# Accumulating transfers, split means and later loads in a hybrid encoder block

## The chip, the cores and the metric

The kernel runs on one NeuronCore of a Trainium2 chip. The metric is the device time of one execution in microseconds. Engines are named as in the profile: PE is TensorE (PEld its weight loads), DVE is VectorE, ACT is ScalarE, POOL is GpSimd and SP is SyncE. SP, ACT and POOL each issue DMA transfers in the order of their own queue, and the 16 DMA engines of the core move the bytes.

## The reference

One layer for 1024 tokens of 1024 channels, all in float32: two token mixers side by side with a gated merge, then a squared-ReLU MLP, with a root-mean-square norm before and after each.

```python
h = rmsnorm(x, g_pre_mix)
u_pool, q, k, v = split(h @ w_in)            # 512 channels each; 8 heads of 64
# pooling: group g of 128 channels, window w = 2, 4, 8, 16
pooled = trailing_mean(u_pool[g], w) - u_pool[g]
y_pool = concat(pooled @ w_pool_mix[g]) * pool_scale @ w_br_pool
# stick-breaking attention, strictly causal
z = q @ k.T / 8
A[t, s] = sigmoid(z[t, s]) * prod(1 - sigmoid(z[t, j]) for s < j < t)
y_sb = (A @ v) @ w_br_sb
gates = sigmoid(h @ w_gate + b_gate)
merged = gates[:, :1024] * y_pool + gates[:, 1024:] * y_sb
x = x + rmsnorm(merged @ w_out, g_post_mix)
h2 = rmsnorm(x, g_pre_mlp)
x = x + rmsnorm(relu(h2 @ w_up) ** 2 @ w_down, g_post_mlp)
```

## The kernel before

**Layout and precision.** Channels lie on the 128 partitions and tokens on the free dimension, in two halves h of 512 tokens. Each float32 operand is split into a high part (a cast, on ACT) and a low part (source minus high part, on DVE), and every product is three matmuls of 128x512 into one PSUM bank: high by high, high by low and low by high (`mm3`, L104 to L106; L102 where attention pins the order).

**Order of the work.** The program is written in one order, and a planner with a cost model of its own fixes each engine's queue at build time: it takes an instruction when, by its reckoning, the operands and the slot are there, so that a queue can differ from the written order. On the chip each queue runs strictly in its fixed order. `issue_after` ties an instruction behind another one of the same engine. Tiles with one tag share a fixed number of slots, and a new tile waits until the old one's readers are through, DMAs among them. The tags m0 to m3 of the pool `mx` are four such slots of 128x1024.

**Stages.** (1) Norm of x, u and v projections. (2) `phase_project`: gates, q and k, twelve pairs of weight blocks, each pair as seven half-size block products (`product`, 12 matmuls) with sums on DVE. `result` ends each block: gates are stored straight from the result's tile on ACT's queue, q and k are scaled and split into a staging tile (slots m0 and m1 in turn) and stored from POOL's queue, q with its high part twice. Beside it runs `later`, advanced by one step per product: per pooling group it loads u, adds up windows on DVE, takes the mean, splits it (`ph`, `pq`), multiplies it and stores the split result; then it prepares v. Partial sums of the down weights are formed in DRAM by copying and accumulating transfers from POOL (`weight_sums`), released a piece at a time: 12 behind u, 16 in the projections, 12 in attention. (3) `phase_attention`: for each half of the tokens (g) eight heads; scores on PE, sigmoid on ACT, a scan on DVE, transposes on PE, a split on ACT and DVE, and products with v. Between them `pump` mixes in other matmul steps, as many per head as `deal` says: `job_pool` (branch product times gate, stored as `bscr`), `job_merge` (the other branch times its gate, plus `bscr`) for the first half, and `job_out`. (4) `phase_post`: `job_merge` for the second half, the out projection, and `chain` beside it: norm, residual added, stored as `xscr`, squares, next norm and the split of the MLP's operands. (5) `phase_mlp`: the up products in two passes; the first stores partial results (`pscr`), the second loads them back in quarters (`quarter`) and combines seven block products per pair of weights (`pair_weights`). `down` does the same with the down weights, loading its first operands early.

## Time and profile before

| What | Value |
|---|---|
| median of three runs | 1279.97 us (1277.24 to 1282.58) |
| profiled execution, its own time | 1283.02 us |
| its span | 1281.1 us |
| instructions | 16198 |
| mean granted TensorE clock | 0.997 |
| bytes moved by DMA | 283 MB |

In rows of instructions an arrow points from the operand to the result ("T<-z" reads z and writes T); a bracket gives the idle time of the engine just before and what ended it. Lines such as L897 are lines of the kernel before. "SPq" and "ACTq" rows are the issue of a DMA. Matmuls are pipelined, so their single durations overlap. A wait for several semaphores is put down to the one that came last.

### The profile page before, as it was taken

To read this page: it belongs to the slowest core of one execution; us is meant where nothing else is said; L and a number is where in the kernel's file an instruction comes from. 1 tells how busy PE (TensorE), PEld (TensorE's weight loads), DVE (VectorE), ACT (ScalarE), POOL (GpSimd) and SP (SyncE) were. 2 spreads that over 40 slices of the span, in tenths; PEclk is the share of its full clock that TensorE was granted. 3 is DMA by queue.
4 is the path that set the end of the run, shared out by engine and by line. 5 is a ranking of instruction groups with operands and counts; after the bars stand their busy time and mean duration, and the time that the engine had idled before them with its cause. 6 is when DMAs were issued, how large, how long until landed. Compare 5 with 4: busy or idle time off the path is not lost.

```text
span 1281.1 us, 16198 instructions
## 1 busy us (share of the span) xinstructions
PE 1247.4 (97%) x5707; PEld 1022.0 (80%) x5707; DVE 970.6 (76%) x1311; ACT 621.9 (49%) x994; POOL 179.3 (14%) x319
## 2 busy tenths in 40 slices
PE   9999989999989999999999999999999999999998
PEld 6887768887877877777778878888888888888887
DVE  8759687776588898777777978888865564776985
ACT  7247344333455556554556635545554443344452
POOL 1212112342101011101101002221221110001000
PEclk9999999999999999999999989999999999999999
DMA  6586878977898774346638756766549997556552
GB/s 217 167 228 173 247 185 252 327 244 240 324 314 315 236 222 137 80 109 220 216 123 286 216 203 224 252 218 242 198 164 318 302 305 241 197 197 246 185 202 67
DMA packets 110306, 283.00 MB, mean 221 GB/s; under 512 B 12465, under 2 KB 17585, under 8 KB 109073
## 3 DMA queue, kind: packets, MB, share of 16 engines
q1 hardware_dynamic: 65696, 165.28, 37.2%
q0 software_dynamic: 30992, 91.13, 25.4%
q10 hardware_dynamic: 13536, 25.57, 6.1%
q8 instruction: 45, 0.74, 0.2%
q14 instruction: 37, 0.29, 0.1%
HBM read 208.52 MB, written 94.37 MB: 236 GB/s over the span
## 4 chain that ended last, share of the span: by engine, by line
PE 59%; DVE 8%; DMA 3%; issue 2%; ACT 2%; ACTq 0%; DVEq 0%; SPq 0%
PE d L104 16%; PE d L106 16%; PE d L105 16%; PE o L830 2%; DVE T L791 2%; PE dbr L106 2%; PE dbr L105 2%; PE dbr L102 2%; PE at L804 2%; DMA wraw<-w 1%; DVE wlo L75 1%; DVE alo L815 1%; DMA gt<-gscr 1%; PE z L787 1%; PE z L784 1%
## 5 line engine op out<-in xcount | busy, mean ns | idle before, releaser
L105 PE MATMUL d<-blo,whi 128*128 128x512 f32 (+1 forms) x456 | 172.3, 378 | 0.0
L106 PE MATMUL d<-bhi,wlo 128*128 128x512 f32 (+1 forms) x456 | 171.9, 378 | 0.0
L104 PE MATMUL d<-bhi,whi 128*128 128x512 f32 (+1 forms) x456 | 168.7, 378 | 0.0
L105 PEld LDWEIGHTS d<-blo,whi 128*128 128x128 f32 x456 | 85.7, 188 | 16.1
L106 PEld LDWEIGHTS d<-bhi,wlo 128*128 128x128 f32 x456 | 85.8, 188 | 15.8
L104 PEld LDWEIGHTS d<-bhi,whi 128*128 128x128 f32 x456 | 85.5, 188 | 16.0
L791 DVE TENSOR_TENSOR_SCAN T<-T,past 128x256 f32<-128x256 f32 (+5 forms) x64 | 84.5, 1347 | 5.8 <-ACT T L789 5.5
L105 PE MATMUL d<-b_lo,whi 128*128 128x512 f32 x196 | 76.3, 390 | 0.5 <-DVE b_lo L1060 0.5
L104 PE MATMUL d<-b_hi,whi 128*128 128x512 f32 x196 | 75.3, 391 | 0.6 <-ACT b_hi L1059 0.6
L106 PE MATMUL d<-b_hi,wlo 128*128 128x512 f32 x196 | 74.8, 390 | 0.0
L75 DVE TENSOR_TENSOR wlo<-wraw,whi 128x1024 fp32r<-128x1024 f32 x45 | 54.9, 1219 | 24.4 <-ACT whi L74 24.4
L74 ACT CAST whi<-wraw 128x1024 fp32r<-128x1024 f32 x45 | 47.4, 1054 | 49.6 <-DMA wraw<-w 17.1
L814 ACT CAST ahi<-at 128x512 fp32r<-128x512 f32 (+1 forms) x96 | 44.6, 483 | 48.5 <-PE at L804 40.2
L815 DVE TENSOR_TENSOR alo<-at,ahi 128x512 fp32r<-128x512 f32 (+1 forms) x96 | 50.7, 549 | 19.8 <-ACT ahi L814 19.5
L1351 DVE TENSOR_TENSOR wlo<-slots_hi,whi 128x1024 fp32r<-128x1024 f32 x29 | 35.5, 1224 | 37.7 <-ACT whi L1349 37.6
L1349 ACT CAST whi<-slots_hi 128x1024 fp32r<-128x1024 f32 x29 | 30.5, 1052 | 68.5 <-PE d L105 62.3
L1349 ACT CAST whi<-slots_lo 128x1024 fp32r<-128x1024 f32 x27 | 28.4, 1054 | 63.4 <-PE d L105 53.1
L104 PE MATMUL sw<-h_hi,whi 128*128 128x512 f32 x144 | 56.5, 393 | 2.0 <-ACT vs L619 0.8
L105 PE MATMUL sw<-h_lo,whi 128*128 128x512 f32 x144 | 56.1, 389 | 0.0
L106 PE MATMUL sw<-h_hi,wlo 128*128 128x512 f32 x144 | 55.5, 390 | 0.1
L104 PE MATMUL d<-t_hi,whi 128*128 128x512 f32 x132 | 52.7, 399 | 2.5 <-ACT whi L1166 2.5
L789 ACT ACTIVATE T<-z 128x256 f32<-128x256 f32 (+3 forms) x96 | 44.3, 500 | 19.9 <-PE z L787 10.9
(443 smaller groups left out, 3425.7 us busy)
## 6 DMA issues: line engine op xcount, KB each, us to landing
wraw<-w SPq DMA_DIRECT2D x57, 512.0 KB, 4.9
ext_b<-ascr SPq DMA_DIRECT2D x40, 512.0 KB, 7.1
wscr<-w POOLq DMA_DIRECT2D x32, 512.0 KB, 8.9
slots_hi<-w SPq DMA_DIRECT2D x10, 1024.0 KB, 7.7
slots_lo<-w SPq DMA_DIRECT2D x10, 1024.0 KB, 8.4
qq<-qscr SPq DMA_DIRECT2D x32, 256.0 KB, 5.9
pscr<-p SPq DMA_DIRECT2D x32, 256.0 KB, 4.5
u<-pscr ACTq DMA_DIRECT2D x32, 256.0 KB, 4.6
```

Source lines behind the costliest of these rows:

```text
L74: nc.scalar.copy(hi, raw)
L75: self.last_lo = nc.vector.tensor_sub(lo, raw, hi.bitcast(F32)).ins
L102: nc.tensor.matmul(ps, wh, rh, start=first and i == 0, stop=False)
L104: nc.tensor.matmul(ps, wh, rh, start=first and i == 0, stop=False)
L105: nc.tensor.matmul(ps, wh, rl, start=False, stop=False)
L106: self.last_mm = nc.tensor.matmul(ps, wl, rh, start=False, stop=last and i == n - 1).ins
L789: self.after = nc.scalar.activation(f, z[:, :n], AF.Sigmoid, scale=-1.0)
L791: nc.vector.tensor_tensor_scan(f[:, ::-1], f[:, ::-1], past[:, ::-1], 1.0, ALU.mult, ALU.max)
L814: nc.scalar.copy(hi[:, c:], at[:, c:])
L815: nc.vector.tensor_sub(lo[:, c:], at[:, c:], hi[:, c:].bitcast(F32))
L1349: last_split[0] = nc.scalar.copy(hi, src).ins
L1351: last_split[1] = nc.vector.tensor_sub(lo, src, hi.bitcast(F32)).ins
```

## The change

- `result`: the high parts of two results of q and k share one staging tile; the low part is written over the result itself, and each part is stored by a transfer of its own (q: six of 128 KB, k: four, for two heads).
- `later`: u of the next group is loaded before the mean is formed; window slots go on alternating over the groups; the mean is split and multiplied in two halves of 512 tokens, each half's parts in one tile; the results are stored from ACT's queue.
- Weight sums: the pieces released in the projections end at the 36th product; four more go to the last heads of attention.
- The first gate tiles of attention are fetched ahead of the y loads.
- `job_merge`: the term from `bscr` is no longer loaded and added on DVE; a transfer from POOL's queue accumulates it into the product's tile. The loads of the second half's gates get other slots, and `deal` changes for the second half.
- `chain`: x is no longer loaded; a transfer from POOL accumulates it into the normed tile, and what follows runs three channels behind.
- `phase_mlp`: quarters 0 and 1 are issued on ACT behind given casts, and the first load of the down operands on SP behind the third pair's weights.

```diff
         self.op7, self.sw, self.heads = {}, {}, {}
+        self.stage = []
         self.phase_in()
...
         sc = sign * (0.125 if kind == "q" else 1.0)
-        e = self.staged([P, 2, H], F32R, f"{kind}s")
-        nc.scalar.activation(e[:, 0, :], t, AF.Copy, scale=sc)
+        if not self.stage:
+            e = self.staged([P, 2, H], F32R, f"{kind}s")
+            self.stage = [e[:, 0, :], e[:, 1, :]]
+        hi = self.stage.pop(0)
+        nc.scalar.activation(hi, t, AF.Copy, scale=sc)
         nc.vector.scalar_tensor_tensor(
-            out=e[:, 1, :], in0=t, scalar=sc, in1=e[:, 0, :].bitcast(F32), op0=ALU.mult, op1=ALU.subtract
+            out=t.bitcast(F32R), in0=t, scalar=sc, in1=hi.bitcast(F32), op0=ALU.mult, op1=ALU.subtract
         )
+        parts = (hi.bitcast(F32), t, hi.bitcast(F32)) if kind == "q" else (hi.bitcast(F32), t)
         for b in range(2):
-            scr, s = self.qscr[kind == "k"][2 * f + b], e[64 * b : 64 * b + 64].bitcast(F32)
-            nc.gpsimd.dma_start(scr[0:128, c].rearrange("(n p) c -> p n c", n=2), s)
-            if kind == "q":
-                nc.gpsimd.dma_start(scr[128:192, c], s[:, 0, :])
+            scr = self.qscr[kind == "k"][2 * f + b]
+            for n, e in enumerate(parts):
+                nc.gpsimd.dma_start(scr[64 * n : 64 * n + 64, c], e[64 * b : 64 * b + 64])
 
...
         yield
+        n = 1
         for g in range(4):
-            iu = 3 * (g % 2)
-            u = nxt_u
-            cur, n = u, 0
+            u = cur = nxt_u
             for i in range(g + 1):
                 sh = 1 << i
-                n = 1 + i % 2
                 nxt = whole(n, name="win")
...
                 nc.vector.tensor_copy(nxt[:, :sh], cur[:, :sh])
-                cur = nxt
+                cur, n = nxt, 3 - n
                 yield
+            if g < 3:
+                nxt_u = u_load(g + 1)
             w = 1 << (g + 1)
...
             sc = self.vt[:, V_PSC + g : V_PSC + g + 1]
-            ph, pq = whole(3 - n, F32R, "ph"), whole(3 - iu, F32R, "pq")
-            nc.scalar.copy(ph, cur)
-            nc.vector.tensor_sub(pq, cur, ph.bitcast(F32))
-            yield
-            yield
-            ds = [self.zps.tile([P, H], F32, name="dm", tag="o", bufs=1), newbank()]
-            for h, d in enumerate(ds):
+            for h in range(2):
                 c = slice(h * H, h * H + H)
-                self.mm3(d, [(wmh[:, g, :], wml[:, g, :], ph[:, c], pq[:, c])])
+                pp = self.mx.tile([P, 2, H], F32R, name="pp", tag=f"m{n}")
+                ph, pq = pp[:, 0, :], pp[:, 1, :]
+                nc.scalar.copy(ph, cur[:, c])
+                nc.vector.tensor_sub(pq, cur[:, c], ph.bitcast(F32))
+                yield
+                d = newbank() if h else self.zps.tile([P, H], F32, name="dm", tag="o", bufs=1)
+                self.mm3(d, [(wmh[:, g, :], wml[:, g, :], ph, pq)])
                 nc.scalar.activation(cur[:, c].bitcast(F32R), d, AF.Copy, scale=sc)
...
                 )
-            if g < 3:
-                nxt_u = u_load(g + 1)
+            yield
             yield
             for t, scr in zip((cur, u), self.yscr):
-                nc.gpsimd.dma_start(scr[:, g, :], t)
-            yield
+                nc.scalar.dma_start(scr[:, g, :], t)
             yield
...
                 next(bg, None)
-            if c % 3 == 2 and c < 48:
+            if c % 3 == 2 and c < 36:
                 self.sum_piece_with(self.last_mm)
...
         self.fetch_order, self.fetches = jobs, {}
+        with tc.issue_after(self.head_load):
+            self.fetch(1)
         last = self.head_load
...
                 if h == 0:
-                    self.fetch(1)
                     self.load_head(1, 0, self.mx)
...
             else:
-                self.fetches[key] = self.staged_in(self.gscr[8 + e][:, c]), self.staged_in(self.bscr[e][h])
+                self.fetches[key] = self.staged_in(self.gscr[8 + e][:, c])
 
...
                 if g or h > 3:
-                    self.sum_pieces(zero, 1)
+                    self.sum_pieces(zero, 1 + (g and h > 3))
             nc.scalar.copy(hi[:, c:], at[:, c:])
...
             self.fetch(self.fetch_order.index(("m", e, 0)) + 1)
-            t, q = self.fetches["m", e, 0]
+            t = self.fetches["m", e, 0]
         else:
-            room = {2: ("T1", 6), 3: ("T0", 5), 4: ("ahi", 4), 5: ("alo", 4)}.get(e)
-            t, q = (self.staged_in(s, room) for s in (self.gscr[8 + e][:, c], self.bscr[e][h]))
+            room = {4: ("T1", 6), 5: ("T1", 6), 6: ("T0", 5), 7: ("T0", 5)}.get(e)
+            t = self.staged_in(self.gscr[8 + e][:, c], room)
         for k in range(4):
...
         nc.vector.tensor_mul(t, t, d)
-        nc.vector.tensor_add(t, t, q)
+        nc.gpsimd.dma_start(t, self.bscr[e][h], accum_op=ALU.add)
         if h not in self.mg:
...
         out = None
-        deal = [[5] * 4 + [4] * 4, [18, 18, 16, 11, 11, 11, 11, 12]]
+        deal = [[5] * 4 + [4] * 4, [16, 16, 14, 12, 12, 12, 13, 13]]
         for g in range(2):
...
         nc = self.nc
-        xr = []
-        for i, n in enumerate(("hi", "lo")):
-            t = self.hp.tile([P, 4, H], F32, name=f"xr{h}_{n}", tag=f"t4_{n}")
-            for j in range(2):
-                (nc.sync if h else nc.gpsimd).dma_start(t[:, 2 * j : 2 * j + 2, :], self.x[h][:, 4 * i + 2 * j : 4 * i + 2 * j + 2, :])
-            xr += [t[:, j, :] for j in range(4)]
         tmp = self.hp.tile([P, 4, H], F32, name=f"tmp{h}", tag="t3_hi")
...
         acc2 = ch.tile([P, H], F32, name="acc2", bufs=1)
-        for e in range(8):
-            yield 6 - early + 3 * e
+        for n in range(11):
+            if n < 8:
+                yield 6 - early + 3 * n
+                m = mix[n]
+
+                with self.tc.issue_after(self.last_lo):
+                    nc.vector.scalar_tensor_tensor(
+                        out=m, in0=m, scalar=self.gn[:, V_POST_MIX + n : V_POST_MIX + n + 1], in1=r,
+                        op0=ALU.mult, op1=ALU.mult,
+                    )
+                nc.gpsimd.dma_start(m, self.x[h][:, n, :], accum_op=ALU.add)
+            e = n - 3
+            if e < 0:
+                continue
             m = mix[e]
-
-            with self.tc.issue_after(self.last_lo):
-                nc.vector.scalar_tensor_tensor(
-                    out=m, in0=m, scalar=self.gn[:, V_POST_MIX + e : V_POST_MIX + e + 1], in1=r,
-                    op0=ALU.mult, op1=ALU.mult,
-                )
-                nc.vector.tensor_add(m, m, xr[e])
             nc.gpsimd.dma_start(self.xscr[h][e], m)
...
             t = big[:, j, :] if i % 2 else self.wp.tile([P, 1024], F32, name="wraw", tag="wraw", bufs=2)
-            self.nc.sync.dma_start(t, self.w[O_UP + f])
+            ins = self.nc.sync.dma_start(t, self.w[O_UP + f]).ins
+            if i == 2:
+                self.third = ins
             raw += [t[:, :512], t[:, 512:]]
...
                 nxt = {"sb": self.pair_b(raw, sums[0], self.wp, "w", 3)}
+                first = self.last_hi
         nxt["a22"] = self.split_weights(raw[3], self.wp, "w", 3)
...
 
-        ps = quarter(0)
+        with tc.issue_after(first):
+            ps = quarter(0)
+        behind = self.last_hi
         for i in range(16):
...
             u, c11 = ps
-            ps = quarter(i + 1)
+            with tc.issue_after(behind) if i == 0 else contextlib.nullcontext():
+                ps = quarter(i + 1)
             v, c22 = buf("v"), buf("c22")
...
 
-        loaded = [None]
+        loaded = [self.third]
 
...
 

```

## The prediction

> **What bounds the kernel now.** I read the profile's busy times first, then the busy time by stage, then who waited for whom on PE, and then the timeline around PE's longest waits. In the stage rows the columns are the stretch, its length, busy time and instructions of PE, PEld, DVE, ACT and POOL, the granted clock, the DMA share and GB/s.
>
> ```profile
> span 1281.1 us, 16198 instructions
> PE 1247.4 (97%) x5707; PEld 1022.0 (80%) x5707; DVE 970.6 (76%) x1311; ACT 621.9 (49%) x994; POOL 179.3 (14%) x319
> ...
> 120.00:200.00 80.00, 74.53 (x321) 59.28 (x320) 64.27 (x94) 33.57 (x46) 10.29 (x13) 1.00 0.79 211
> 200.00:300.00 100.00, 98.06 (x431) 80.27 (x429) 71.78 (x104) 36.53 (x51) 34.88 (x60) 1.00 0.88 279
> 300.00:340.00 40.00, 38.23 (x167) 31.35 (x168) 27.31 (x38) 17.74 (x23) 7.97 (x14) 1.00 0.72 247
> 340.00:436.00 96.00, 90.72 (x472) 75.33 (x472) 75.57 (x110) 51.19 (x124) 10.12 (x32) 1.00 0.87 311
> 460.00:480.00 20.00, 17.71 (x95) 14.57 (x94) 19.21 (x25) 10.51 (x23) 2.29 (x5) 1.00 0.75 218
> 480.00:500.00 20.00, 18.46 (x98) 14.93 (x97) 18.73 (x21) 13.03 (x27) 2.50 (x5) 1.00 0.63 180
> 540.00:560.00 20.00, 17.54 (x93) 14.05 (x92) 15.50 (x19) 13.40 (x28) 1.41 (x3) 1.00 0.34 75
> 580.00:620.00 40.00, 39.42 (x171) 31.61 (x171) 29.15 (x44) 14.37 (x23) 2.48 (x5) 1.00 0.59 190
> 620.00:660.00 40.00, 38.92 (x166) 30.65 (x166) 35.63 (x52) 26.59 (x44) 3.24 (x6) 1.00 0.58 199
> 660.00:740.00 80.00, 78.38 (x344) 63.99 (x342) 63.51 (x91) 45.52 (x74) 4.32 (x8) 1.00 0.72 237
> 740.00:760.00 20.00, 19.06 (x70) 15.02 (x71) 11.80 (x16) 6.15 (x8) 0.00 (x0) 0.83 0.52 183
> 760.00:940.00 180.00, 180.00 (x796) 149.05 (x795) 151.10 (x219) 98.69 (x152) 37.66 (x70) 1.00 0.63 217
> 940.00:1240.00 300.00, 300.00 (x1325) 248.40 (x1324) 201.69 (x209) 129.11 (x147) 24.33 (x34) 1.00 0.77 248
> ```
>
> TensorE is the bound: 1247.4 of 1281.1 us. The change leaves its matmuls as they are, so it can only win back what PE loses: 33.7 us of idle time, plus what slower clock costs. From 760 to 1240 PE loses nothing, and nothing done there can be won. The losses lie in four places: 9.2 us in the projections (5.47 + 1.94 + 1.77, from 120 to 340), 5.3 us in the first half of attention, in its second half among others 2.3 and 1.5 us (460 to 500, where DVE is busy 19.21 and 18.73 of 20) and 2.5 us (540 to 560, where it is not), and about 6 us around 740. There the granted clock is 0.83: 70 matmuls in 20 us, where 180/796 = 0.226 us each would make 88. The missing 18 cost 4.2 us, and the 660 to 740 row has another 1.6 us of idle time, nearly all just before 740. This sum is made against the profiled execution's own 1283.0 us (the span and 1.9 us around it), which is 3.0 us above the median of the three runs.
>
> **Projections, pooling.** Two waits of DVE (who waited for what, us in total, times, longest), and one of its instructions:
>
> ```profile
> DVE win L575 <- DMA yscr<-win: 8.2, 3, 6.7
> DVE win L575 <- DMA u<-uscr: 3.9, 1, 3.9
> ...
> 168.57 1.22 DVE L589 TENSOR_TENSOR pq<-win,ph 128x1024 fp32r<-128x1024 f32 x1
> ```
>
> DVE first stands 12.1 us on pooling's own stores and loads, and then does windows and weight splits in a heap, so that PE's weights and banks come late. After, the first window of a group goes into the slot of the split operands (free after a product), not into the one being stored, and u is loaded before the products, not behind them. Both waits go. The split by halves costs 0.15 us per group (two of some 0.69 for one of 1.22) and makes the second half wait for the first half's product, which shares its slot. The eight stores pass from POOL to ACT's queue behind two more steps, so ACT does not wait for DVE there. Of the 5.5 us I take half, 2.5; the ends are 0 and 4 (the rest is weight splitting, which stays).
>
> **Projections, low parts in place.** The timeline around the longest of PE's waits, POOL's issues, the landing times, and two later waits of DVE:
>
> ```profile
> 298.33 0.63 ACT L536 ACTIVATE ks<-v 128x512 fp32r<-128x512 f32 x1 [3.16 <-DMA qscr<-ks]
> 298.99 0.69 DVE L537 SCALAR_TENSOR_TENSOR ks<-v,ks 128x512 fp32r<-128x512 f32 x1 [3.10 <-ACT ks L536]
> 300.94 0.50 PE L104 MATMUL sw<-ht_hi,a1hi 128*128 128x512 f32 x1 [2.59 <-DVE u L699]
> ...
> L544 POOL DMA_DIRECT2D qscr<-qs x16: 521/533/594, 219.4 to 283.7; - x16
> ...
> qscr<-qs POOLq DMA_DIRECT2D x16, 256.0 KB, 4.7
> qscr<-qs POOLq DMA_DIRECT2D x16, 128.0 KB, 5.1
> ...
> 342.05 0.69 DVE L690 TENSOR_TENSOR v<-u,sw 128x512 f32<-128x512 f32 x1 [6.31 <-DMA gscr<-v]
> 351.29 0.69 DVE L897 TENSOR_TENSOR gt<-gt,dbr 128x512 f32<-128x512 f32 x1 [4.07 <-DMA gt<-gscr]
> ```
>
> A store of k holds the staging tile; ACT, then DVE, then PE's bank wait for it in a chain. With the high parts of two results in one tile, and the low part in the result's own tile, a tile is asked for half as often, and this wait goes: 2.6 us. What is late next is the result's tile, since the next pair writes v only when its store has landed; five products (60 matmuls, 13.6 us) lie between, against some 3.2 us of POOL issues (6 x 0.53) and 5 us of landing. The issues rise from 48 to 80: 32 x 0.53 = 17 us more on POOL, which is busy 34.88 of 100 us there and gives up its accumulations of weights from the 36th product on. I take a gain of 2 (ends +4 and -2.6).
>
> Here a rule of the Trainium skill speaks against the change: the page DMA: Bandwidth & Descriptors, section Rules for kernel authors, wants many small transfers made into one large one and finds no use in splitting by partition halves. The two landing rows agree that half the bytes land no sooner. By it alone the 32 more transfers could only lose, and the time would be the third rival's below.
>
> **Attention.** DVE's 4.07 us for the first gate tile precede the first gaps of PE there. The fetch now goes ahead of the y loads, which gives 1.5 of the 5.3 us; the y loads move back by two of 256 KB, some 1.7 us at the 311 GB/s of that stretch, and no row has PE waiting for them. In the second half:
>
> ```profile
> L918 DVE TENSOR_TENSOR gt<-gt x12: 666/686/694, 440.6 to 610.4; 128x512 f32<-128x512 f32 x12
> ...
> slots_hi<-xscr POOLq DMA_DIRECT2D x4, 256.0 KB, 5.1
> xr<-xscr POOLq DMA_DIRECT2D x8, 256.0 KB, 7.0
> slots_hi<-w POOLq DMA_DIRECT2D x4, 1024.0 KB, 15.7
> ```
>
> Eight merges there lose an add of 0.686 us: 5.5 us off a DVE that is nearly full from 460 to 500, where PE loses 3.8. The new deal gives the last five heads one step more each (3 matmuls, 0.68 us), where PE idles with DVE free, and takes two from each of the first three. POOL gets the accumulation behind the product, and what is queued behind it there (weight loads, memsets, weight sums) waits for that product; POOL is busy 2.5 of 20 us, so I cost this at nothing, and at 3 us if the order is bad. I take -3 (ends +3 and -6).
>
> An accumulation into SBUF of 256 KB has no row. Plain loads of its size from POOL land in 5.1 and 7.0 us, the 1 MB accumulation in 15.7. I take 6, near its own size, and keep 5 and 16.
>
> **Merges' end and residuals.**
>
> ```profile
> 604.89 0.68 DVE L917 TENSOR_TENSOR gt<-gt,d 128x512 f32<-128x512 f32 x1
> ...
> 610.42 0.68 DVE L918 TENSOR_TENSOR gt<-gt 128x512 f32<-128x512 f32 x1
> 611.02 1.46 DVE L925 TENSOR_TENSOR mg_lo<-gt,mg_hi 128x512 fp32r<-128x512 f32 x2
> ...
> 625.15 1.29 DVE L1090 TENSOR_TENSOR mix<-mix,xr_lo 128x512 f32<-128x512 f32 x2
> ...
> 641.16 0.69 ACT L143 ACTIVATE rb<-ms,eps 128x512 f32<-128x512 f32 x1 [1.57 <-PE ms L1099]
> ```
>
> Today the last merge's product is multiplied at 604.9 and added only at 610.42, since DVE's queue is full; 0.68 for it, 0.53 of issue and 6 of landing end at 612.1 against 611.1 today, and all eight gates have room of their own, so the multiplication can come some 2 us sooner. Even. The residual adds (16 x 0.686 = 11 us of DVE) go; the last three channels follow the last accumulation without a step between, some 3 us after today's last add at 626.4 if it lands in 6, but the sum at 641 stands 14 us behind that add, so it is covered up to a landing of about 13 us. From 580 to 740 I take -1 (ends +4 and -2).
>
> **Quarters later.**
>
> ```profile
> 730.89 5.62 DMA wraw<-w
> ...
> 732.70 0.85 ACTq L1236 DMA_DIRECT2D u<-pscr  x2
> 736.54 0.69 DVE L1175 TENSOR_TENSOR sums<-wraw 128x512 f32<-128x512 f32 x1 [2.67 <-DMA wraw<-w]
> 740.89 0.79 PE L104 MATMUL d<-t_hi,whi 128*128 128x512 f32 x1 [2.51 <-ACT whi L1166]
> ...
> 744.00:746.00 2.00, 2.00 (x6) 0.50 1.00 408
> ```
>
> PE waits for the first weights of the second pass: their load lands 5.6 us after its issue, DVE waits 2.67 us for it, and PE then stands 2.51 us and runs at half clock after. Quarter loads (512 KB at 732.7) share that stretch of DMA. Moved behind the splits they free some 1.3 us at 400 GB/s and its load lands in 4.3 instead of 5.6. I expect PE's wait at 0.5 to 1.5 us and no half clock: -5 of the 6 (ends 0 and -6). The first use of a quarter is behind a product of 2.7 us and has the other banks to cover it.
>
> The clock's threshold is not certain: PE's 2.59 us at 298 left the clock at 1.00, the 2.51 us here did not. The Trainium skill's page TensorE: Matmul & The Clock Gate, section HAM oscillation, allows gaps up to about 3.4 us. By that no half clock would belong here, and 3.4 us less could be won; the row shows 0.50, so the row decides.
>
> **Sum.** -2.5 - 2 - 1.5 - 3 - 1 - 5 = -15: 1283 - 15 = **1268 us**.
>
> **Rivals.**
> - *The load at 730 stays late.* Two other quarters are not held back and may go first; then PE still stands 2 us and half clock follows: 1268 + 5 = 1273.
> - *The freed DVE time is filled by latency:* attention and post give nothing, as idle time at 540 to 560 shows that a free DVE alone does not fill PE: 1268 + 5.5, and up to 3 more from POOL's order: 1273 to 1277.
> - *Stores hold the results.* If POOL's 80 issues run late, v waits for its store as at 342; with 2.6 us of PE for each of the four q and k pairs, 1268 + 10 = 1278.
> - *Slower: accumulations land like the 1 MB ones,* in 16 us. The last merge is then ready at 605 + 0.7 + 0.5 + 16 + 1.4 = 624 instead of 612.5; PE finds other products while merges are late (0.6 us idle from 580 to 620), which I take to cover half of these 11.5 us, and stands 5 to 6; the same lateness at the first merges costs another 5; the sum at 641 comes 3 us late and the second stand brings 3.4 us of half clock. With 17 us back and only 9.5 won in projections and at 740: 1283 - 9.5 + 17 = 1290. It decides from a landing of about 13 us. Against it: the two rows of 256 KB.
>
> **Chances.** Forecast 0.50 (its own range 1262 to 1273), late load 0.16, latency 0.13, stores 0.08, slower 0.13. Three runs of the kernel can tell about 0.5%, 6.4 us of 1280, from no change; faster means under 1273.6, slower over 1286.4. Faster: 0.49 of the forecast, 0.10 of the late load and 0.04 of latency, 0.63. Slower 0.13. Same 0.24. The range goes from 1258 (all ends at their best but one) to 1284.
>
> **What would show it.** Right: no wait of DVE for pooling's stores or of ACT for k's store; DVE below 18 of 20 us after 460; a granted clock of 1.00 from 740 to 760 and 88 matmuls there; accumulations landing in 5 to 7 us. Wrong: PE waiting for the high part of a merge after 612, for the statistics at 641, or at 740 for the same load.

## The result and the profile after

The changed kernel is slower: 1320.95 us median (1319.54 to 1323.10, four runs) against 1279.21 (1277.24 to 1282.58, four runs), a ratio of 1.0325 with a 95% interval of 1.0297 to 1.0353. That is 41.6 us lost, where the prediction's sum won 15. Below, a ratio is turned into us by multiplying its distance from 1 by 1280.

The head of the profile after, stages of it by the same columns as before (stretch, length, busy time and instructions of PE, PEld, DVE, ACT and POOL, granted clock, DMA share, GB/s), and PE's longest waits (total, times, longest):

```profile
span 1317.8 us, 16208 instructions
PE 1259.6 (96%) x5707; PEld 1030.2 (78%) x5707; DVE 956.2 (73%) x1283; ACT 623.7 (47%) x998; POOL 214.8 (16%) x371
...
120.00:200.00 80.00, 72.82 (x307) 58.49 (x306) 57.43 (x84) 30.97 (x44) 7.70 (x8) 0.96 0.78 192
200.00:300.00 100.00, 90.16 (x384) 73.22 (x383) 72.20 (x105) 36.97 (x51) 38.52 (x71) 0.95 0.72 225
300.00:370.00 70.00, 61.08 (x250) 49.23 (x249) 37.80 (x53) 20.71 (x29) 16.09 (x30) 0.93 0.71 249
490.00:510.00 20.00, 17.00 (x75) 13.70 (x75) 16.11 (x19) 10.36 (x23) 3.20 (x8) 0.83 0.73 209
510.00:530.00 20.00, 18.28 (x99) 15.28 (x98) 16.82 (x19) 12.08 (x27) 3.01 (x6) 1.00 0.49 145
640.00:660.00 20.00, 16.55 (x60) 11.87 (x59) 12.47 (x18) 9.67 (x17) 8.78 (x12) 0.88 0.88 225
970.00:1270.00 300.00, 300.00 (x1325) 248.40 (x1324) 203.83 (x213) 131.30 (x151) 27.10 (x39) 1.00 0.76 250
```

```profile
PE sw L104 <- DVE v L692: 13.4, 3, 7.6
PE d L104 <- ACT whi L74: 5.6, 3, 3.0
PE sw L104 <- ACT s1hi L1170: 4.4, 1, 4.4
```

Where the 36.7 us between the two spans went: DVE has 14.4 us less to do (956.2 for 970.6), just as intended, and PE's matmuls are the same 5707. PE is idle for 58.2 us instead of 33.7 (24.5 more) and busy for 12.2 us more, since after each long stand the clock is granted at half. Set against the same numbered matmul of before, the kernel is 25 us late at the 1600th (381 us of before, where the projections are done), 30 at the 2700th (605), 37 at the 2900th (654), 36.5 at the last. So two thirds are lost in the projections, some 5 us in attention and 7 at the merges' end and the residuals. From the second pass on nothing is lost or won: 1325 matmuls in 300 us, as before.

What the change set out to remove is gone. The wait of DVE for pooling's stores, 8.2 us before, is down to the first row here, and its 3.9 us for u are no longer among its waits. The accumulations land as assumed, with a 256 KB median of 4.5 us for a merge and 7.7 for a residual:

```profile
  DVE win L577: 0.7, 1
...
gt<-bscr POOLq DMA_DIRECT2D x12, 256.0 KB, 4.5
mix<-x POOLq DMA_DIRECT2D x16, 256.0 KB, 7.7
```

### The profile page after: what moved, and what is told of

It is laid out like the page before. It is cut to its first block, busy times and chain, and to the rows that moved or that the text cites. A ratio compares the mean times of both kernels' runs of the same rounds, so it can differ in the third digit from the quotient of the medians.

```text
span 1317.8 us, 16208 instructions
## 1 busy us (share of the span) xinstructions
PE 1259.6 (96%) x5707; PEld 1030.2 (78%) x5707; DVE 956.2 (73%) x1283; ACT 623.7 (47%) x998; POOL 214.8 (16%) x371
## 3 DMA queue, kind: packets, MB, share of 16 engines
q0 software_dynamic: 34384, 93.23, 27.1%
## 4 chain that ended last, share of the span: by engine, by line
PE 55%; DVE 7%; issue 7%; DMA 6%; POOL 2%; ACT 1%; ACTq 0%; SPq 0%; DVEq 0%; POOLq 0%
PE d L104 14%; PE d L106 14%; PE d L105 14%; DMA mix<-x 2%; PE dbr L105 2%; PE dbr L106 2%; PE o L833 2%; PE dbr L102 2%; PE at L807 1%; DMA vpair<-vscr 1%; DVE T L794 1%; DMA gt<-bscr 1%; PE sw L104 1%; PE sw L105 1%; PE sw L106 1%
## 5 line engine op out<-in xcount | busy, mean ns | idle before, releaser
L1170 ACT CAST whi<-wraw 128x1024 fp32r<-128x1024 f32 (+1 forms) x29 | 26.8, 931 | 60.2 <-PE sw L105 13.6
```

The costliest lines, as they stand in the source:

```text
L1170: self.last_hi = nc.scalar.copy(hi, src).ins
```

## The experiments

**The parts alone.** Each run is the kernel before with one part of the change. First pooling (windows in other slots, u a group ahead, halves, stores by ACT), and then q and k:

```diff
+            u = cur = nxt_u                      # u loaded ahead of the products
+            for h in range(2):
+                pp = self.mx.tile([P, 2, H], F32R, name="pp", tag=f"m{n}")   # both halves: one slot
...
+                nc.scalar.dma_start(scr[:, g, :], t)                         # was nc.gpsimd
```

> Only the pooling part of the change (u a group ahead, means split and multiplied by halves, results stored from ACT's queue); all else as before. In the traces of before and after, the same matmul (number 900, at 219 us before) comes 5.4 us later after the change, and at that place little but the pooling part has run. Theory A, each part brings waits of its own: 1279 + 5 = 1284 us, with the delay in place by 220 us and none added between 220 and 340. Theory B, the parts only hurt together, because a shifted pooling pushes the q, k and v work into a worse order: the delay grows behind 220 us as in the changed kernel, 1279 + 5 + 15 = 1299 us. If my prediction's step were right: 1276.5 us.

> Only the part on q and k (high parts of two results in one staging tile, low part over the result, each part stored by its own transfer, 80 instead of 48 issues from POOL), with the move of four weight sums that belongs to it. Between matmul 900 and matmul 1400 the changed kernel loses 19.4 us on the kernel before. Theory A, the waits are this part's own (v's preparation stores from POOL's queue behind 32 more issues, DVE stands for v's next load, PE for DVE's queue behind it): 1279 + 19 = 1298 us, with DVE's waits for v's load at some 19 us in sum and two or three stretches of half clock between 220 and 340. Theory B, they come from the order that pooling leaves: within 4 us of 1279. The rival of the prediction, results waiting for their own stores: waits of DVE for stores of q and k, some 10 us.

Pooling alone takes 1293.96 us, ratio 1.0097 (1.0079 to 1.0115): 12.4 us slower, between the two theories. Its profile is 9.6 us behind at the 900th matmul and 17.6 at the 1600th, so the delay grows behind 220 us without q and k too. q and k alone take 1274.74, ratio 0.996 (0.9941 to 0.9979): 5.1 faster. In that profile ACT's waits for stores of the staging tile, before it writes a high part, fall from 15.9 us to 2.5, and PE is 2.8 us ahead at the 1600th matmul, near the 2 that were forecast; the run also moves four weight sums into attention, so what the new stores give by themselves is not separated. The 19 us that PE falls behind in the changed kernel while q and k are made are not theirs alone.

The first stand of pooling's run can be read off four rows; the first row of the fence is from the kernel before:

```profile
126.02 0.69 ACT L596 ACTIVATE win<-sw,vt 128x512 fp32r<-128x512 f32 x1
...
138.12 0.62 ACT L1164 CAST a0hi<-wrawx 128x512 fp32r<-128x512 f32 x1 [8.85 <-DMA wrawx<-w]
138.65 0.68 ACT L596 ACTIVATE win<-sw,vt 128x512 fp32r<-128x512 f32 x1
141.91 0.75 DVE L597 SCALAR_TENSOR_TENSOR u<-sw,vt,win 128x512 fp32r<-128x512 f32 x1
142.71 0.50 PE L104 MATMUL sw<-ht_hi,a1hi 128*128 128x512 f32 x1 [3.17 <-DVE u L597]
```

The product of pooling's second half lies in a projection's bank `sw`. Before, ACT took it out at 126.02, ahead of the cast of the weights a0, which waits for its load. With the halves one behind the other, it comes 12.6 us later, behind that cast; DVE follows, and PE stands for the bank, and then runs at half clock.

The merges, the residuals and the two moves (fetch and quarters):

```diff
-        nc.vector.tensor_add(t, t, q)
+        nc.gpsimd.dma_start(t, self.bscr[e][h], accum_op=ALU.add)      # e3_merge, with slots and deal
...
-                nc.vector.tensor_add(m, m, xr[e])
+                nc.gpsimd.dma_start(m, self.x[h][:, n, :], accum_op=ALU.add)   # e4_chain, 3 channels' lag
...
+        with tc.issue_after(self.head_load):                            # e5_late
+            self.fetch(1)
...
+        with tc.issue_after(first):
+            ps = quarter(0)
```

> Only the merges (the bscr term accumulated by a transfer from POOL, the gates' slots, and the new deal for the second half of attention). The changed kernel loses 5 us in attention and 9.3 us between matmuls 2700 and 2800, where merges and residuals stand side by side. Theory A, the accumulation's landing (4.5 to 7.2 us) stands in front of the high part on ACT and of what is queued behind it on ACT and DVE: 1279 + 5 + 6 = 1290 us, PE's waits at the end of the merges by 6 us longer than before. Theory B, the nine us at the end come of the residuals sharing POOL's queue: 1279 + 5 = 1284 us, none at the end.

> Only the residuals (x accumulated into the normed tile by a transfer from POOL, what follows three channels behind). Theory A, landings of 7.7 us are covered by the three channels and by PE's other products, as the sum came in time in the changed kernel: 1279 us within 2. Theory B, the squares wait for landings in ACT's queue and hold the casts of weights behind them, so that PE waits around 620 to 660: 1279 + 5 = 1284 us, with waits of ACT for the accumulated tile of 10 us and more.

> The two moves alone: the fetch of the first gates ahead of the y loads, and the quarters (and the other loads of the second pass) held back; everything else as before. Theory A, the prediction's: the first weights of the second pass land earlier, PE's wait at 740 (2.51 us before) falls to 0.5 to 1.5 us, no half clock follows: 5 us off for the quarters and 1.5 for the fetch, about 1274 against 1280. Theory B, the late load has another cause (DVE's and ACT's queue ahead of the split): PE still stands over 2 us there, with or without half clock, and the time is within 2 us of before.

Merges: 1288.31, ratio 1.0047 (1.0026 to 1.0068), 6.0 us slower; PE is 4.2 us behind at the 2600th matmul and 10.7 at the 2800th, so both attention and the merges' end lose, as in theory A. Residuals: 1290.66, ratio 1.0066 (1.0041 to 1.0092), 8.4 slower. The moves: 1280.22, ratio 0.9991 (0.9975 to 1.0008), no change that can be told. In its one profile the stand at 740 falls from 2.51 to 1.73 us and the clock stays at 1.00, which is nearer theory A, but the medians of ten and thirteen runs give 1 us, theory B's time.

How a residual's landing reaches PE, in the run of the residuals alone (POOL, ACT, PE):

```profile
615.34 0.54 POOL L1090 DMA_DIRECT2D xscr<-mix  x1 [0.54 <-DMA mix<-x]
615.87 2.70 POOL L1085 DMA_DIRECT2D mix<-x  x3
...
621.85 0.63 ACT L1092 ACTIVATE tmp<-mix 128x512 f32<-128x512 f32 x1 [6.14 <-DMA mix<-x]
...
625.37 1.03 ACT L74 CAST whi<-wraw 128x1024 fp32r<-128x1024 f32 x1
...
626.45 0.80 PE L104 MATMUL d<-mg_hi,whi 128*128 128x512 f32 x1 [5.29 <-ACT whi L74]
```

POOL accumulates three channels, stores three (each store waits for a landing), and only then accumulates the next three at 615.87. ACT waits 6.14 us for the first of these, and 1.7 us more for the next two. Behind its squares stands the cast of the next weights, for which PE stands 5.29 us.

**Do the parts add up?** Pooling with q and k, and the change without pooling:

> Pooling's part and the q and k part together, nothing else. Alone they gave +13.7 and -5.6 us. Theory A, they are independent: about +8, 1288. Theory B, they add up badly, as the shift in the changed kernel suggests (+30 us at the 2100th matmul, where pooling alone has +16 and q and k alone -5): +25 or more, 1305, with an 8 us stand of PE near 259 behind a weight load and a value load that DVE's fixed order puts ahead of a combination.

> The changed kernel with pooling as before; every other part of the change is in. Theory A, pooling in company with q and k is the largest loss, and the rest adds up as alone (q and k -5.6, merges +7, residuals +9, the moves 0): +8 to +14, about 1290. Theory B, the parts of the second half add up badly too (PE stood 24 us later per the shift between the 1400th and the last matmul in the changed kernel): +18 or more.

Together, pooling and q and k take 1305.30, ratio 1.0194 (1.0170 to 1.0218): 24.8 us slower, where their sum is 7.3. Without pooling the change takes 1289.28, ratio 1.0057 (1.0039 to 1.0076): 7.3 slower, theory A's side, and the sum of the other parts is -5.1 + 6.0 + 8.4 - 1.2 = 8.1. So by these times everything adds up but pooling: it costs 12.4 us alone and 41.6 - 7.3 = 34.3 in the changed kernel, and the company of q and k is 17.5 of the 21.9 us between.

One thing blurs these sums: a part's time also holds what happens far from its edit. Eight runs edit nothing behind attention (pooling and q and k, alone and together, and five of those below), and in all eight PE's stand at 740 is gone or short: 0.2 to 1.1 us between the starts of two matmuls, for 2.90 before, with the clock at 1.00. PE's first matmul of the second pass in pooling's run, and in that of pooling with q and k:

```profile
753.77 0.39 PE L104 MATMUL d<-t_hi,whi 128*128 128x512 f32 x1
766.11 0.50 PE L104 MATMUL d<-t_hi,whi 128*128 128x512 f32 x1 [0.75 <-ACT whi L1168]
```

Set against the profile of before, these runs regain 4.3 to 7.5 us between the 2800th and the 3300th matmul. In seven of them the planner has put the matmuls from 690 to 735 us in another order; in the eighth (pooling with q and k) it has not. In its own stretch, up to the 1600th matmul, pooling is 17.6 us late and q and k 2.8 us early, and the two together are 27.1 late: 12.3 worse than their sum, where the times say 17.5. Seven runs that edit only what comes after the projections lie from 0.7 us ahead to 2.6 behind there, which is how far one profile can be trusted.

The mechanism of the changed kernel's longest stand, from two profiles. DVE's rows of the q and k run, and then DVE's and PE's of the changed kernel, at the same place of the program:

```profile
241.48 1.22 DVE L1171 TENSOR_TENSOR s1lo<-wrawx,s1hi 128x1024 fp32r<-128x1024 f32 x1
...
243.99 0.69 DVE L694 TENSOR_TENSOR v<-u,sw 128x512 f32<-128x512 f32 x1
...
249.22 0.69 DVE L1171 TENSOR_TENSOR a0lo<-wrawx,a0hi 128x512 fp32r<-128x512 f32 x1 [0.83 <-ACT a0hi L1170]
```

```profile
254.86 1.23 DVE L1171 TENSOR_TENSOR s1lo<-wrawx,s1hi 128x1024 fp32r<-128x1024 f32 x1
...
263.48 0.69 DVE L1171 TENSOR_TENSOR a0lo<-wrawx,a0hi 128x512 fp32r<-128x512 f32 x1 [6.79 <-ACT a0hi L1170]
264.21 0.69 DVE L514 TENSOR_TENSOR wrawx<-wrawx 128x512 f32<-128x512 f32 x1
264.97 0.69 DVE L618 TENSOR_TENSOR vpair<-vpair 128x512 f32<-128x512 f32 x1
...
266.18 0.68 DVE L692 TENSOR_TENSOR v<-u,sw 128x512 f32<-128x512 f32 x1
...
267.00 0.77 PE L104 MATMUL sw<-ht_hi,s1hi 128*128 128x512 f32 x1 [7.63 <-DVE v L692]
```

In both, the split of s1 frees the slot into which the next weights are loaded, so that a0 can be split six or seven us later. In the first, the planner has put eight other DVE instructions into that time, among them the sum v that gives PE a bank. In the changed kernel v stands behind a0 and behind the values' vpair: DVE idles 6.79 us, and PE stands 7.63. DVE had nothing too much to do there; the new order puts the instruction that frees a bank behind one that waits for a load.

**What in pooling.** Four runs take its steps apart, and one changes the bank.

```diff
-                d = newbank() if h else self.zps.tile([P, H], F32, name="dm", tag="o", bufs=1)
+                d = self.zps.tile([P, H], F32, name="dm", tag="o", bufs=1)      # e8_obank, in e1_pool
...
+            for h, sl in enumerate((3 - n, 3 - iu)):                             # e13_halves: split alone,
+                pp = self.mx.tile([P, 2, H], F32R, name="pp", tag=f"m{sl}")      # a slot for each half
...
-                nc.scalar.dma_start(scr[:, g, :], t)
+                nc.gpsimd.dma_start(scr[:, g, :], t)                             # e15_poolstore, in e1_pool
...
-                nc.gpsimd.dma_start(scr[:, g, :], t)
+                nc.scalar.dma_start(scr[:, g, :], t)                             # e19_actst, in before
```

> Pooling's part alone (+13.7 us), with one thing changed: the second half's product goes into the bank of the first half instead of one of the projections' banks. In the profile of pooling's part alone ACT copies that bank out behind a weight cast that waits 8.85 us for its load, and PE then stands 3.56 us for the bank (139 us) and 5.32 at 161. Theory A, the projections' bank held behind ACT is the loss: the stands at 139 and 161 go or fall under 1 us, and the time is within 3 us of before (1277 to 1283). Theory B, pooling's heavier order on DVE and ACT makes the weights late whatever bank is used: the stands stay and the time is 1290 or more.

1289.65, ratio 1.0066 (1.0041 to 1.0091), 8.4 us slower. Theory A's stands at 139 and 161 did go, and by the 800th matmul this run is 3.8 us ahead of before. But others come for them:

```profile
PE sw L104 <- DVE v L688: 10.0, 3, 6.8
PE dm L104 <- ACT pp L591: 4.4, 1, 4.4
```

PE stands 4.4 us for a half's operand, whose windows DVE makes too late for the place that the product has in PE's queue, and 10.0 us for v, 6.8 of them at 316 behind a load of values. So the bank is a cause of the early stands, and of no more than some 4 us of the time.

> Pooling split by halves alone, each half with a slot of its own, u loaded and results stored as before. Pooling's whole part cost 12 to 14 us; its last product moved from 199 to 201 us to 218 to 224. Theory A, the split itself (the second half's split and product behind the first's) makes pooling long: the last product is at 210 or later and the time +6 to +14. Theory B, the slot that the halves share and u a group ahead do it: the last product stays within 5 us of 201 and the time within 3 us of before.

> Pooling's whole part (+13.7 us alone), with its eight result stores issued by POOL as before, not by ACT. Theory A, the loss comes from the slot that the two halves share, with u a group ahead: pooling's last product stays near 218 us instead of 201, the values' preparation starts late, and the time is +9 to +15. Theory B, ACT's queue, where the stores now stand among weight casts, is the loss: the time is within 4 us of before.

> The kernel before with its eight pooling result stores issued by ACT, one step later, instead of by POOL; nothing else. Theory A, ACT's queue is a bad place for them by itself: +5 to +10. Theory B, it hurts only where pooling ends late and meets the values' loads in the same queue: within 3 us of before.

The split alone: 1280.53, ratio 1.0000 (0.9984 to 1.0016). Theory B's time, although the last product comes at 209 rather than 201; in place it costs 4.4 us (at the 1600th matmul of its profile), which come back around 740. The whole part with POOL's stores: 1285.58, ratio 1.0030 (1.0019 to 1.0042), 3.8 us slower; its last product ends as late as in pooling's own run (221 and 224 us), so lateness is not what costs the rest. ACT's stores alone: 1275.93, ratio 0.9974 (0.9958 to 0.9991), 3.3 us *faster*. So no single step is to blame: the stores win 3.3 us alone and cost 8.6 with the other steps of pooling (12.4 - 3.8).

```diff
# e16_qhalves: e2_qk with the edit of e13_halves;  e18_afterpool: the changed kernel with the edit of e15_poolstore
```

> The q and k part (-5.6 us alone) with pooling split by halves in two slots (0 alone). Theory A, the bad company of q and k with pooling (+24 us together) is pooling's lateness, which this form of pooling does not have: -7 to -2 us. Theory B, any heavier order of pooling on ACT and DVE meets q and k's stores badly: +5 or more.

> The changed kernel with one thing undone: pooling's eight result stores are issued by POOL, not by ACT. Alone that took pooling's part from +13 to +4 us. Theory A, the stores on ACT's queue are also what makes pooling with q and k so bad: 1321 falls by 20 or more, to 1300 or less, and PE's 8 us stand at 259 goes. Theory B, they cost the same in company as alone: about 1311. Theory C, in company the lateness itself decides: 1317 or more.

q and k with the split: 1282.23, ratio 1.0010 (0.9993 to 1.0027), between the theories: 0 and -5.1 make +1.3, with a new stand of 5.3 us for a half's operand at 142. The changed kernel with POOL's stores: 1316.71, ratio 1.0292 (1.0263 to 1.0321), only 4.2 us better, between theories B and C: the stand near 260 is shorter (3.7 us between two matmuls for 8.0), and others are longer. What rule of the order makes pooling and q and k cost 17.5 us more than apart is thus shown for one stand and not settled for the rest; whether the slots m0 to m3, which q, k, pooling and the values share, decide it, no run tests.

**Residuals: queue, landing or latency?** Three variants of the residuals alone:

```diff
-        for n in range(11):
+        for n in range(13):
...
-            e = n - 3
+            e = n - 5                                      # e9_lag5
...
-            nc.gpsimd.dma_start(self.xscr[h][e], m)
+            nc.scalar.dma_start(self.xscr[h][e], m)        # e14_actstore
...
-            nc.scalar.activation(sq, m, AF.Square)
+            nc.gpsimd.tensor_mul(sq, m, m)                 # e12_poolsq, and the sum: nc.gpsimd.tensor_add
```

> The residuals' accumulations alone (+9 us), with the store and the square of a channel five channels behind its accumulation instead of three. In the profile with three, POOL issues the accumulations of channels 3 to 5 at 615.87, though their products are done at 612.56, because the stores of channels 0 to 2 stand ahead in its queue and wait for landings; ACT then waits 6.14 us for channel 3 with a weight cast behind the square, and PE stands 5.68 us. Theory A, that queue is the loss: with five, the accumulations issue some 3 us earlier, PE's stand at 621 falls to 2 us or less, and the time is +1 to +4 of before. Theory B, the landing itself (6.6 us) in front of ACT's in-order queue is the loss: the stand only moves, and the time stays +7 to +10.

> The residuals' accumulations alone, with the stores of the finished channels issued by ACT, just ahead of their squares, instead of by POOL. POOL then issues all eight accumulations without a store between. Theory A, POOL's queue is half of the loss: the accumulations of channels 3 to 5 issue at about 612 instead of 615.87, ACT's wait for channel 3 falls from 6.14 to 2 or 3 us, PE's stand at 621 to 2 us or less, and the time is +1 to +4. Theory B, the landings get slower when more are under way, so that the channels come no earlier: the stand stays near 5 us and the time +7 to +10.

> The residuals' accumulations alone, with the squares and their sum on POOL instead of ACT and DVE, so that neither of these two waits for a landing any more. The kernel computes the same. Theory A, the wait for landings in ACT's in-order queue, with a weight cast behind it, is what stops PE (5.68 us at 621, 5.09 with a lag of five): that stand goes, with its half clock, and the time is -4 to +2 of before. Theory B, the latency of the chain itself counts: PE stands at the statistics instead (641 and 700), by 4 us or more, and the time is +5 or more.

With a lag of five: 1290.18, ratio 1.0070 (1.0043 to 1.0096). POOL's queue came out in the same order, three accumulations, three stores, three accumulations at 614.66, so this run says nothing on theory A: the program's order is not the queue's order. With ACT's stores: 1291.19, ratio 1.0081 (1.0054 to 1.0109). POOL now issues the second three at 608.29, and theory B holds: ACT gets them some 1.8 us apart from 617.13 on (its stores are issued as each lands), and PE stands 4.8 us as before. The queues' rows (packets, MB, share of 16 engines' time) from 602 to 623 us show why; in that stretch the first is all accumulations, the second all stores of the same channels:

```profile
q0 software_dynamic: 864, 1.57, 44.0%
q10 hardware_dynamic: 864, 1.57, 20.8%
```

```profile
617.13 0.33 ACTq L1090 DMA_DIRECT2D xscr<-mix  x1
617.50 0.63 ACT L1092 ACTIVATE tmp<-mix 128x512 f32<-128x512 f32 x1 [3.86 <-DMA mix<-x]
619.02 0.33 ACTq L1090 DMA_DIRECT2D xscr<-mix  x1
619.40 0.63 ACT L1092 ACTIVATE tmp<-mix 128x512 f32<-128x512 f32 x1 [1.26 <-DMA mix<-x]
620.74 0.33 ACTq L1090 DMA_DIRECT2D xscr<-mix  x1
```

For the same bytes an accumulation takes 2.1 times the DMA engines' time: 0.44 x 21 us / 6 = 1.54 us of all sixteen for 256 KB, beside 0.73 for a store. POOL's queue is not the reason: in the kernel before, where POOL issues the stores of `xscr`, they take 0.68 (23.1% of 20 us for 1.78 MB, from 612 to 632 us).

With squares and sums on POOL: 1300.21, ratio 1.0158 (1.0130 to 1.0186), 20.2 us slower. Both theories are right, one after the other. PE's waits from 595 to 760 us, then a DVE group of this run and of the residuals' own (600 to 660 us; line, shapes, count, busy, mean ns):

```profile
PE d L104 <- ACT whi L1165: 9.7, 1, 9.7
PE d L106 <- DVE wlo L75: 4.9, 3, 3.0
PE ms L158 <- ACT acc_hi L156: 4.7, 1, 4.7
```

```profile
L933 DVE TENSOR_TENSOR acc<-acc,sq 128x512 f32<-128x512 f32 x7 | 10.4, 1486 | 0.1
...
L933 DVE TENSOR_TENSOR acc<-acc,sq 128x512 f32<-128x512 f32 x6 | 4.1, 687 | 0.4 <-ACT sq L931 0.3
```

The stand behind the squares has gone (at 618 two matmuls are 2.0 us apart, for 5.7). But the chain is as long as it was and POOL is slow at it: PE stands at the statistics (ms) and for the first weights of the second pass. And while POOL computes, an add of DVE takes longer: of the seven in the first row, the four that ran beside an instruction of POOL took 1.53 to 3.27 us, and the three beside none 0.68 to 0.69.

**Merges with a lag.**

```diff
+        self.lag.append((e, t))
+        while len(self.lag) > (2 if e < 7 else 0):
+            i, s = self.lag.pop(0)                 # the split of merge i, two merges later
```

> The merges' accumulation alone (+7 us), with ACT's and DVE's split of a merge written two merges behind its accumulation, the last three in a heap. Theory A, the loss is the landing (5.7 us) that stands in front of ACT's and DVE's in-order queues: with two merges between, ACT's waits for landings (11.4 us in three, 595 to 665) fall under 6 us, and the time is +0 to +3 of before. Theory B, the loss is the last merge's own landing and the dealt order in attention, which the lag leaves as they are: the stands of PE at 475 and 608 to 613 stay and the time is +5 to +9.

1284.24, ratio 1.0032 (1.0017 to 1.0048): 4.1 us slower, 2 less than without. ACT's wait for landings is still 9.9 us in three; the last merges have no merge behind them that could cover them. Theory B is nearer, and half of it: PE's stand near 475 stays at 2.9 us, the one near 610 is shorter.

**What the runs point to.** The parts that were not slower alone:

> The q and k part with the fetch and the quarters' moves: all parts that were not slower alone. Theory A, they add up: -5.6 and 0, about 1274, 0.994 to 0.997 of before. Theory B, the moves bring the 3.9 us that their profile showed: 1270 to 1272, below 0.994.

1272.82 us (1270.90 to 1278.59, six runs), ratio 0.9942 (0.9921 to 0.9962): 7.4 us faster than before, on the border of the two theories, and by the two ratios 3.7% below the changed kernel. Its page, and two stages of it:

```profile
PE 1242.1 (98%) x5707; PEld 1020.7 (80%) x5707; DVE 971.7 (77%) x1311; ACT 621.7 (49%) x994; POOL 193.4 (15%) x351
...
200.00:300.00 100.00, 99.48 (x439) 82.08 (x439) 78.42 (x112) 39.91 (x55) 46.00 (x85) 1.00 0.82 259
740.00:760.00 20.00, 20.00 (x90) 16.57 (x89) 17.72 (x26) 9.17 (x13) 1.08 (x2) 1.00 0.59 218
```

From 200 to 300 us PE does 439 matmuls for 431, and the 740 to 760 row has a clock of 1.00 and 90 matmuls, where the prediction asked for 88. That second row does not show that the moves did it, since the eight runs above have no half clock there without them.

## Why the prediction was wrong

By its own steps:

| Step | Predicted | Alone | What the runs showed |
|---|---|---|---|
| Pooling | -2.5 (0 to -4) | +12.4 | wrong sign; +34.3 in company |
| q and k | -2 (+4 to -2.6) | -5.1 | right sign; 2.8 of it in the projections |
| Fetch and quarters | -6.5 | -1.2 (-3.2 to +1.0) | a shorter stand in the profile, as in runs without them; small in the medians |
| Attention's second half, merges | -3 (+3 to -6) | +6.0 | wrong sign, beyond the end |
| Merges' end, residuals | -1 (+4 to -2) | +8.4 | wrong sign, beyond the end |

*Pooling is the step that failed.* The two waits that it was to remove went, and its 12.1 us of standing DVE with them. The prediction then priced the split by halves at DVE's 0.15 us a group, and put two things at nothing: that it "makes the second half wait for the first half's product", and the stores' move to ACT's queue. The ends 0 to -4 had no loss in them at all. In place of -2.5 the part measured +12.4 alone. The second half did come late, and its bank, a projection's, was then released behind a cast that waits for a load; but with another bank 8.4 of the 12.4 us stay, and with the stores back on POOL 3.8. The loss is thus one of several steps that meet in fixed queues. The rows show it for two stands of PE, at 142 us alone and at 267 in the changed kernel; the cause of the rest stays open.

*Adding the terms is the second.* The sum took each part's gain from the profile of before, as if the order around it stayed. By the times, 21 of the 41.6 us are in no part alone; in their own stretch, up to the 1600th matmul, pooling and q and k are 12.3 us worse together than apart. The planner orders all queues anew, and a bank that PE needs came to stand behind a load.

*Covered is the third.* The sum at 641, which "stands 14 us behind that add, so it is covered up to a landing of about 13 us", did come in time: in the residuals' run its matmul waits for nothing. But that looked at who uses the sum. What was hit was a weight cast behind the squares in ACT's in-order queue. The landing of 6 us was about right (medians of 4.5 for the merges and 7.7 for the residuals); its price was not, and neither was the slower rival's: that one needed landings of 13 us, and 256 KB never took so long in the median. Three accumulations at a time also land one behind the other, some 1.8 us apart, which one landing time does not show.

*The rival "the freed DVE time is filled by latency" came true in attention, and more than that was lost:* at 490 to 530 DVE is busy 16.11 and 16.82 of 20 us, below the 18 that were to show the step right, and PE's 17.00 (at a clock of 0.83) and 18.28 are no better than 17.71 and 18.46. By that rival attention wins nothing; the merges alone lost 6.0 us.

*The quarters* were to leave a PE wait of 0.5 to 1.5 us and a clock of 1.00. In the moves' own profile it is 1.73, in the run of the good parts none, and the clock is 1.00 in both. But the largest term of the sum, -5, rested on a stand that one profile of before shows and that edits elsewhere remove as well; that the moves shorten it is not shown. In the changed kernel PE still stands 2.68 us for the first weights, the row that was to show the step wrong, but with the clock at 1.00. Another such row, PE waiting for the high part of a merge, is there too: 2.0 us in two, the longest 1.84 us at 634.76.

```profile
778.95 0.50 PE L104 MATMUL d<-t_hi,whi 128*128 128x512 f32 x1 [2.68 <-ACT whi L1170]
...
778.00:782.00 4.00, 2.53 (x10) 1.78 (x11) 2.95 (x3) 3.34 (x5) 0.00 (x0) 1.00 0.69 205
```

*The range and a detail.* From 1283 the best ends of the terms add up to 1260.9 and the worst to 1292.5, where the range has 1258 and 1284; the slower rival's 1290 lay outside it, and the measured time lies beyond all of them. The new deal gives the last five heads six steps more (1, 1, 1, 2, 1), not one each.

*The rule on small transfers* (the Trainium skill, page DMA: Bandwidth & Descriptors, section Rules for kernel authors) was weighed as a reason why q and k's 32 more transfers could only lose. The measurement decides against it here: alone that part is 5.1 us faster, and ACT waits 13.4 us less for stores of the staging tile.

## What to carry to other kernels

When an add is turned into a transfer, cost it not by who uses the sum but by what stands behind the first instruction that waits for the landing, on each in-order queue. When a part is split in two, ask where its second half's bank is released, and behind which load. Where a planner fixes the queues, time the parts alone and together before believing a sum: here the parts that were good alone made 7.4 us, and the whole lost 41.6. Compare the profiles stretch by stretch as well: a new order can win or lose time where nothing was edited.

## What was not expected of the hardware

- *Half clock.* In the twenty profiles of this case, with a stand of PE of 3.7 us or more between the starts of two matmuls (0.23 us of it the matmul's own), half clock began in the stand or within 2.5 us behind it in 23 of 23 cases; from 3.0 to 3.65 us in 12 of 17, from 2.2 to 3.0 in 15 of 32, and below, from 1.5 to 2.2, in 6 of 104. Its stretches in the changed kernel last 3.4, 6.8 or 10.2 us. The Trainium skill's page TensorE: Matmul & The Clock Gate, section HAM oscillation, puts the limit near 3.4 us; above it the traces agree, below it half clock is frequent all the same.
- *Accumulating transfers* of 256 KB into SBUF cost the DMA engines 2.1 times what a store of the same bytes does (1.54 us of all sixteen for 0.73).
- *POOL and DVE.* DVE's add of two SBUF tiles took 1.53 to 3.27 us in place of 0.69 while POOL multiplied and added. The Trainium skill's page SBUF — State Buffer, section Who interferes with whom, says that a DVE instruction with two SBUF inputs contends with a GpSimd one that reads SBUF; the trace agrees.
